# A transformer block on one core: the order of its first loads, and of its first pass over the grid

## The chip, the core and the metric

The kernel runs on one core of one Trainium2 chip. A core has five engines that run beside each other, each through its own list of instructions in order: PE (TensorE, matrix products into the PSUM accumulators), DVE (VectorE), ACT (ScalarE), POOL (GpSimd) and SP (SyncE, which here only starts transfers). Transfers between the chip's memory and the core's own SBUF are started from SP's, ACT's or POOL's list and then run on 16 DMA engines. The metric is the device time of one execution in microseconds (us), the median over several runs.

## What is computed

One layer of a diffusion backbone: 1024 tokens of 1024 features (a grid of 16 rows by 64 columns), 256 context tokens, float32 throughout. Cut to what the change touches:

```python
shift, scale, gate = adaln(c, w_ada, b_ada)          # silu(c) @ w_ada + b_ada, cut in three
shift_c, scale_c, gate_c = adaln(c_ctx, w_ada, b_ada)
h = rmsnorm(x, norm_g) * (1 + scale[:, None]) + shift[:, None]
hc = rmsnorm(ctx, norm_g) * (1 + scale_c) + shift_c
q, k, v, za, u, bg, cg, zc = jnp.split(h @ w_in, SPLIT_POINTS, axis=-1)
...
x_new = x + gate[:, None] * (jnp.concatenate([attn, conv], axis=-1) @ w_out)
```

`w_ada` is 1024 x 3072 and `w_in` 1024 x 4096. The left out lines hold a windowed attention with rotary positions and a gated short convolution.

## The kernel before

The 1024 features lie in 8 *feature tiles* of 128. Everything ahead of the first accumulator's end is called the opening here; both the change and the prediction concern it alone.

**Operands in two parts.** For float32 accuracy at the matrix unit's quicker rate, each operand of a large product is split into a high part (ACT copies it, rounding) and a low part (DVE subtracts). A product is then three matmuls: high by high, high by low, low by high. `split` does this for a slab of `w_ada`, `chunk_split` and `split_chunk(k)` for a chunk of `w_in`, `modulated` for `h`.

**adaLN.** `w_ada`'s shift and scale columns are loaded in *slabs* of 1024 rows by 256 columns, 1 MB each: `load_slab(m, j)` for m = 0..3 and j = 0 (shift) or 1 (scale). A slab pair m covers the feature tiles 2m and 2m + 1. `products(m, j)` multiplies `silu(c)` and `silu(c_ctx)` (`c2`, two columns) with a slab; for m = 0 and 1 in plain float32, which PE runs in two passes, so that one such matmul shows as two rows in the profile; for m = 2 and 3 in split form. The outcome lies in one partition per condition. `row_copy` brings it to SBUF, `modulation(m, rw)` turns it with eight small matmuls against `comb` ("turns") into a column per feature, and three DVE operations add the biases and write `ab`, the shift and scale per feature.

**x.** `load_x` loads row tiles of 128 tokens, 0.5 MB each, `xx[0..7]`; tiles 0 to 3 are *half 0* of the grid, 4 to 7 half 1. Each tile gets `square` (ACT, sum of squares), `root` (a small DVE operation, then POOL's power) and `norm` (DVE). `transposed(half, k)` turns feature tile k of four row tiles on PE into one of two `tr` banks, and `turn(half, k, engine)` applies `ab` and writes `h`'s two parts: ACT writes the high part, ACT or DVE the full value `hw`, DVE the low part.

**The first pass over the grid.** `first_columns(half, k)` multiplies chunk k of `w_in` (three columns blocks of 128) with feature tile k of one half: nine matmuls of 512 columns into three accumulators of that half. There are six accumulator banks (`acc0[u][half]`) and two `tr` banks, which fill the eight banks of PSUM. In before, the pass goes through both halves for each pair of feature tiles.

**What sets the order.** During the opening every engine, and SP with its transfers, is held to the order in which the code is written (`strict`). So an instruction that waits holds up all that is written behind it on its engine. Transfers issued from ACT or POOL are outside this rule but still stand in those engines' lists. In before SP's loads are, in order: vec and ci (the small constants and the identity), slab pair 0 in halves, x tiles 0 to 3, chunk 0, x tiles 4 to 7, chunk 1, slab pair 1, chunks 2 and 3, slab (2,0). Slabs from m = 1 on share three slots, with x's context tile `xc`, the table inputs `rw8` and the rotary table `rg` behind them; `rg` (four POOL operations in `gains`) takes the slot of slab (3,1), so it waits for the last `split`. SP stores `rg`, loads chunks for the next stage behind it, then the bias tables, then the weights `uraw`.

Of the kernel before, what the change touches and what calls it, by code (L numbers as in the profile page):

```python
# [10 lines left out]
F32 = mybir.dt.float32  # L11
# [3 lines left out]
ALU = mybir.AluOpType  # L15
# [4 lines left out]
P = 128  # L20
# [19 lines left out]
def body(tc, es, x, ctxt, w_ada, b_ada, w_in, q_g, k_g, rpbr, w_out, vecs, cst, out):  # L40
# [74 lines left out]

    vec = cp.tile([P, P], F32, name="vec")
    nvec = vecs.shape[0]
    sp.dma_start(vec[:nvec], vecs)
    sp.dma_start(ci, cst[:, 0:P + 2])
    few = cp.tile([P, 8], F32, name="few")  # L120
    pool.memset(few[:, 0:4], -0.5)
    pool.memset(few[:, 4:5], 1.0)
# [18 lines left out]
    def place(k, shape, dtype, name):  # L141

        return hpool.tile(shape, dtype, name=name, tag=f"h{k}")
# [377 lines left out]
    def tr():  # L521
        return ps0.tile([P, 512], F32, name="tr", tag="tr", bufs=2)
# [4 lines left out]
    def load_x(ts):  # L527
        for t in ts:
            xx[t] = xp.tile([P, D], F32, name="xx", tag="xx", bufs=8)
            sp.dma_start(xx[t], x[0, t * P:(t + 1) * P])  # L530

    def load_slab(m, j):

        new = place(6 + j, [P, KT, 256], F32, "slab") if m == 0 else sl.tile([P, KT, 256], F32, name="slab", tag="slab", bufs=3)
        n = 2 if m == 0 else 1
        for i in range(n):
            rows = slice(KT // n * i, KT // n * (i + 1))
            sp.dma_start(new[:, rows], bass.AP(w_ada.tensor, w_ada.offset + j * D + 256 * m + 3 * D * P * rows.start,
                                               [[3 * D, P], [3 * D * P, KT // n], [1, 256]]))
        slabs[m, j] = new  # L540

    def load_chunks(ks):
        for k in ks:
            chunks[k] = chunk_load(CU, k)

    load_slab(0, 0)
    load_slab(0, 1)
    load_x(range(4))
    load_chunks([0])
    load_x(range(4, 8))  # L550
    load_chunks([1])
# [9 lines left out]
    pv = tr()  # L561
# [32 lines left out]
    def products(m, j, kts=range(KT)):  # L594

        if m not in mods:
            mods[m] = tr()
        rows = mods[m][:2 if m < 2 else 4, 256 * j:256 * j + 256]
        parts = [(c2, slabs[m, j])] if m < 2 else [(c4, highs[j]), (c4, lows[j])]
        for i, (c, part) in enumerate(parts):  # L600
            for kt in kts:
                pe.matmul(rows, c[:, kt], part[:, kt], start=(i == 0 and kt == 0 and j == 0),
                          stop=(i == len(parts) - 1 and kt == KT - 1 and j == 1), skip_group_check=True)

    def row_copy(m):
        n = 2 if m < 2 else 4
        rw = cvp.tile([4, 512], F32, name="rw", tag="ub", bufs=2)
        act.copy(rw[:n], mods[m][:n])
        return rw[:n]

    def modulation(m, rw):
# [12 lines left out]
        dve.tensor_tensor(abk[:, 1], abk[:, 1], both(ng), ALU.mult)  # L624
# [90 lines left out]

    more_h(range(6))

    products(0, 0)
    products(0, 1)
    for t in range(4):  # L720
        square(xx[t], t)
    root(0)
    root(1)
    norm(xx[0], 0)
    root(2)
    norm(xx[1], 1)
    root(3)
    norm(xx[2], 2)
    rw = row_copy(0)
    modulation(0, rw)  # L730
    norm(xx[3], 3)
    transposed(0, 0)
    transposed(0, 1)
    square(xx[4], 4)
    root(4)
    split_chunk(0)
    turn(0, 0, dve)
    square(xx[5], 5)
    norm(xx[4], 4)
    root(5)  # L740
    turn(0, 1, dve)
    first_columns(0, 0)
    square(xx[6], 6)
    norm(xx[5], 5)
    root(6)
    square(xx[7], 7)
    norm(xx[6], 6)
    root(7)
    split_chunk(1)
    norm(xx[7], 7)  # L750
    first_columns(0, 1)
    products(1, 0, range(4))
    transposed(1, 0)
    turn(1, 0, act)
    products(1, 0, range(4, KT))
    load_slab(2, 1)
    load_chunks([4, 5])
    transposed(1, 1)
    products(1, 1)
    load_slab(3, 0)  # L760
    split_chunk(2)
    turn(1, 1, act)
    first_columns(1, 0)
    rw = row_copy(1)
    split_chunk(3)
    split(2, 0, 0)
    load_slab(3, 1)
    load_chunks([6, 7])
    transposed(0, 2)
    modulation(1, rw)  # L770
    turn(0, 2, dve)
    split(2, 0, 1)
    split(2, 1, 0)
    split(2, 1, 1)
# [3 lines left out]
    transposed(1, 2)  # L778

    for m in range(1, 4):  # L780
# [10 lines left out]
        if m == 1:  # L791
            split(3, 0, 0)
            split(3, 0, 1)
            tables = gains_load()
# [24 lines left out]
        if new:  # L819
            split_chunk(k + 3)  # L820
        if m == 1:
            split(3, 1, 0)
# [11 lines left out]
        if m == 1:  # L834
            split(3, 1, 1)
# [588 lines left out]
```

## Time and profile before

| | us |
|---|---|
| median of 3 runs | 655.83 (655.49 to 657.02) |
| profiled execution: span, first to last instruction | 653.6 |
| span not covered by the median | 2.2 (655.83 - 653.6) |
| mean granted TensorE clock over the span | 0.995 |

The profiled execution has no separate time beside its span. The profile's page gives busy time by engine, the chain of waits that ended last, and groups of instructions; a window gives busy time of each engine in a stretch of the span, the clock granted to PE, the share of the 16 DMA engines that was busy, and GB/s. A row of the timeline has start, duration, engine, line, operation, the tile written and the tile read, a count, and in brackets the idle time of the engine before it with what ended it. Nearly all rows carry line 55, a helper that records every operation, so groups are told apart by tile names: `tr`, `acc`, `xx`, `sqj` (squares), `xss` (roots), `slab`, `slabh`, `slabl`, `wr`, `wh`, `wl`, `rw`, `ab`, `h`, `hw`. PE is matmuls, PEld the loading of the stationary operand.

### The profile page before, as it was taken

The numbers are of one execution on the slowest core, as the hardware profiler recorded it, in microseconds if no ns is written. First come the engines' busy times: TensorE is split into PE (matmuls) and PEld (weight loads), VectorE is DVE, ScalarE is ACT, GpSimd is POOL, SyncE is SP. The second block draws the span as 40 slices with busy tenths as digits, with TensorE's granted clock in tenths as the row PEclk, the third lists the DMA queues.
The fourth block names the chain that finished last, engine by engine and source line by source line (L and its number), as shares of the span: only waits on it lengthen the run. The fifth ranks groups of instructions, "written<-read, shape, count | busy, mean of one in ns | idle before, by whom it ended". The sixth has DMA issues, their size and how long they took to land.

```text
span 653.6 us, 10275 instructions
## 1 busy us (share of the span) xinstructions
PE 628.5 (96%) x3469; PEld 539.0 (82%) x3469; DVE 431.8 (66%) x814; ACT 322.1 (49%) x693; POOL 129.7 (20%) x137
## 2 busy tenths in 40 slices
PE   5899998999899999999999999999999999999997
PEld 1567798999699999977878888888888888888885
DVE  1567664866584856457786989988998864575111
ACT  3566643442543534427677647565685654342000
POOL 1204102312222222101111211111211210104421
PEclk9799999999999999999999999999999999999999
DMA  8863647686586799789949586877782223966621
GB/s 320 311 210 134 169 117 232 201 259 202 143 266 196 247 276 261 188 221 215 238 106 234 143 200 174 224 188 165 212 193 78 73 74 104 316 225 206 207 100 51
DMA packets 118865, 125.46 MB, mean 192 GB/s; under 512 B 32818, under 2 KB 89354, under 8 KB 117533
## 3 DMA queue, kind: packets, MB, share of 16 engines
q1 hardware_dynamic: 112348, 113.23, 60.3%
q10 hardware_dynamic: 6208, 11.05, 5.4%
q0 software_dynamic: 256, 0.54, 0.3%
q8 instruction: 27, 0.44, 0.3%
q14 instruction: 26, 0.20, 0.1%
HBM read 88.01 MB, written 38.53 MB: 194 GB/s over the span
## 4 chain that ended last, share of the span: by engine, by line
PE 70%; DMA 10%; DVE 7%; SPq 5%; ACT 3%; issue 2%; POOL 1%; ACTq 0%; DVEq 0%; POOLq 0%
PE pu L55 20%; PE pacc L55 17%; PE po L55 5%; PE pout L76 4%; PE pout L74 4%; PE pout L75 4%; SPq L55 3%; DMA k_s<-k_d 3%; PE cacc L55 3%; PE tr L55 3%; PE pss L55 2%; PE pmx L55 2%; DMA v<-v_d 2%; DMA xx<-in_x 2%; DVE mx L55 1%
## 5 line engine op out<-in xcount | busy, mean ns | idle before, releaser
L55 PE MATMUL pu<-h,uh 128*128 128x512 f32 x544 | 169.0, 392 | 0.0
L55 PE MATMUL pacc<-wh,h 128*128 128x384 f32 x512 | 135.5, 338 | 0.6 <-ACT qn L55 0.6
L55 PEld LDWEIGHTS pu<-h,uh 128*128 128x128 f32 x544 | 98.2, 188 | 17.0
L55 PE MATMUL pu<-h,ul 128*128 128x512 f32 x272 | 106.3, 391 | 0.0
L55 PEld LDWEIGHTS pacc<-wh,h 128*128 128x128 f32 x512 | 92.9, 188 | 1.0 <-ACT qn L55 1.0
L55 POOL TENSOR_TENSOR plc<-sc,phc 128x512 fp32r<-128x512 f32 x32 | 42.4, 1324 | 222.1 <-ACT sc L55 120.0
L55 PE MATMUL pacc<-wl,h 128*128 128x384 f32 x256 | 85.6, 334 | 0.0
L55 POOL TENSOR_TENSOR ss<-ss,few 128x4 f32<-128x4 f32 (+1 forms) x40 | 41.9, 1050 | 131.6 <-DVE ss L55 131.3
L55 PEld LDWEIGHTS pu<-h,ul 128*128 128x128 f32 x272 | 51.1, 188 | 11.3
L55 DVE TENSOR_TENSOR mx<-mx,sb 128x384 f32<-128x384 f32 (+1 forms) x64 | 55.8, 880 | 2.0
L75 PE MATMUL pout<-wol,yh 128*128 128x512 f32 x128 | 49.8, 389 | 0.0
L76 PE MATMUL pout<-woh,yl 128*128 128x512 f32 x128 | 49.6, 389 | 0.0
L55 DVE TENSOR_REDUCE ss<-sq 128x4 f32<-128x260 f32 (+1 forms) x40 | 15.8, 394 | 50.3 <-ACT sq L55 50.2
L74 PE MATMUL pout<-woh,yh 128*128 128x512 f32 x128 | 48.3, 389 | 0.0
L55 PEld LDWEIGHTS pacc<-wl,h 128*128 128x128 f32 x256 | 48.1, 188 | 0.1
L55 ACT COPY mg<-pmx 128x256 f32<-128x256 f32 x32 | 12.0, 374 | 58.3 <-PE pmx L55 47.4
L55 ACT ACTIVATE sq<-pacc 128x256 f32<-128x256 f32 x32 | 12.3, 385 | 53.0 <-PE pacc L55 52.2
L1356 DVE TENSOR_TENSOR ot<-pout,gate 128x512 f32<-128x512 f32 x16 | 10.8, 688 | 38.4 <-PE pout L76 36.3
L55 DVE TENSOR_TENSOR pll<-sb,phl 128x768 fp32r<-128x768 f32 (+2 forms) x33 | 29.3, 889 | 7.9 <-ACT sb L55 7.9
L1357 POOL TENSOR_TENSOR ot<-ot,xr 128x512 f32<-128x512 f32 x15 | 20.1, 1344 | 68.2 <-DVE ot L1356 67.3
L55 DVE TENSOR_TENSOR sc<-sc,mg 128x512 f32<-128x512 f32 x32 | 21.8, 683 | 17.4 <-ACT mg L55 17.4
L55 ACT ACTIVATE qn<-pacc,ss 128x64 f32<-128x64 f32 x128 | 29.9, 327 | 6.4 <-POOL ss L55 3.2
(146 smaller groups left out, 1273.9 us busy)
## 6 DMA issues: line engine op xcount, KB each, us to landing
uraw<-in_w_in SPq DMA_DIRECT2D x34, 256.0 KB
q_d<-qs SPq DMA_DIRECT2D x64, 128.0 KB
k_s<-k_d SPq DMA_DIRECT2D x16, 512.0 KB
q_s<-q_d SPq DMA_DIRECT2D x32, 256.0 KB
wr<-in_w_in SPq DMA_DIRECT2D x40, 192.0 KB
slab<-in_w_ada SPq DMA_DIRECT2D x6, 1024.0 KB
t_d<-btw SPq DMA_DIRECT2D x8, 576.0 KB
bt<-t_d SPq DMA_DIRECT2D x8, 576.0 KB
```

What stands on the lines that cost most here:

```text
L55: i = emit(*a, **kw)
L74: i = pe.matmul(ps, ah, bh, start=first, stop=False)
L75: pe.matmul(ps, ah, bl, start=False, stop=False)
L76: pe.matmul(ps, al, bh, start=False, stop=last)
L1356: dve.tensor_tensor(ot, ps, gate[:, cols], ALU.mult)
L1357: (dve if (nh, t) == (1, NB - 1) else pool).tensor_tensor(ot, ot, xr, ALU.add)
```

## The change

Four things.

- vec and ci are loaded through ACT's list instead of SP's, and SP begins with x tiles 0 to 3.
- Slab pair 0 is loaded by feature tile: for k = 0 and 1 the shift and scale columns of that tile alone, two pieces of 0.5 MB with rows of 512 bytes instead of 1024. Products, row copy and modulation of pair 0 are done for each of the two tiles by itself (`first_products`, `first_row`, `first_modulation`). x tiles 4 to 7 come behind slab pair 1.
- The products of the pairs 0 and 1, and the first small transpose, no longer use the `tr` banks but accumulator banks of half 1, which the grid pass needs later.
- The grid pass takes half 0 through the feature tiles 0 to 3, then half 1 through the same four, and goes on as before from feature tile 4. `split_chunk`, `split`, the later loads and the squares are placed anew within that order.

```diff
-    sp.dma_start(vec[:nvec], vecs)
-    sp.dma_start(ci, cst[:, 0:P + 2])
+    act.dma_start(vec[:nvec], vecs)
+    act.dma_start(ci, cst[:, 0:P + 2])
...
+    def load_first_slabs(k):
+
+        both = place(6 + k, [P, 2, KT, P], F32, "slab")
+        for j in range(2):
+            sp.dma_start(both[:, j], bass.AP(w_ada.tensor, w_ada.offset + j * D + P * k,
+                                             [[3 * D, P], [3 * D * P, KT], [1, P]]))
+        slabs[k] = both
...
-    load_slab(0, 0)
-    load_slab(0, 1)
     load_x(range(4))
-    load_chunks([0])
-    load_x(range(4, 8))
-    load_chunks([1])
+    for k in range(2):
+        load_first_slabs(k)
+        load_chunks([k])
     load_slab(1, 0)
     load_slab(1, 1)
-    load_chunks([2, 3])
+    load_chunks([2])
+    load_x([4, 5])
+    load_chunks([3])
+    load_x([6, 7])
     load_slab(2, 0)
...
+    def first_products(k, j):
+
+        ps = mods[k] = acc0[1 - k][1]
+        for kt in range(KT):
+            pe.matmul(ps[:2, P * j:P * j + P], c2[:, kt], slabs[k][:, j, kt], start=(j == 0 and kt == 0),
+                      stop=(j == 1 and kt == KT - 1), skip_group_check=True)
+
+    def first_row(k):
+        rw = cvp.tile([4, 512], F32, name="rw", tag="ub", bufs=2)
+        act.copy(rw[:2, :256], mods[k][:2, :256])
+        return rw[:2]
...
```

The order of the opening after the change, as it is written (`first_modulation` is `modulation` for one feature tile, with four turns and three DVE operations of half the size):

```python
    for t in range(3):
        square(xx[t], t)
        root(t)
        if t:
            norm(xx[t - 1], t - 1)
            transposed(0, 0, [t - 1])
            transposed(0, 1, [t - 1])
    square(xx[3], 3)
    root(3)
    norm(xx[2], 2)
    norm(xx[3], 3)
    first_products(0, 0)
    transposed(0, 0, [2])
    transposed(0, 1, [2])
    first_products(0, 1)
    transposed(0, 0, [3])
    transposed(0, 1, [3])
    rw = first_row(0)
    split_chunk(0)
    first_modulation(0, rw)
    turn(0, 0, dve)
    first_products(1, 0)
    first_products(1, 1)
    first_columns(0, 0, (0,))
    rw = first_row(1)
    split_chunk(1)
    first_columns(0, 0, (1,))
    first_modulation(1, rw)
    turn(0, 1, dve)
    products(1, 0)
    load_slab(2, 1)
    load_chunks([4, 5])
    products(1, 1)
    load_slab(3, 0)
    square(xx[4], 4)
    root(4)
    split_chunk(2)
    square(xx[5], 5)
    norm(xx[4], 4)
    root(5)
    first_columns(0, 0, (2,))
    transposed(0, 2)
    first_columns(0, 1, (0,))
    rw = row_copy(1)
    norm(xx[5], 5)
    split_chunk(3)
    modulation(1, rw)
    turn(0, 2, dve)
    first_columns(0, 1, (1, 2))
    transposed(0, 3)
    square(xx[6], 6)
    root(6)
    turn(0, 3, act)
    first_columns(0, 2)
    square(xx[7], 7)
    norm(xx[6], 6)
    root(7)
    split(2, 0, 0)
    norm(xx[7], 7)
    split(2, 0, 1)
    transposed(1, 0)
    turn(1, 0, act)
    first_columns(0, 3)
    transposed(1, 1)
    split(2, 1, 0)
    split(2, 1, 1)
    turn(1, 1, act)
    load_slab(3, 1)
    load_chunks([6, 7])
    first_columns(1, 0)
    transposed(1, 2)
    ...
    turn(1, 2, act)
    products(2, 0)
    first_columns(1, 1)
    split(3, 0, 0)
    split(3, 0, 1)
    tables = gains_load()
    split_chunk(4)
    products(2, 1)
    rw = row_copy(2)
    transposed(1, 3)
    first_columns(1, 2, (0,))
    modulation(2, rw)
    turn(1, 3, act)
    split_chunk(5)
    split(3, 1, 0)
    first_columns(1, 2, (1, 2))
    transposed(0, 4)
    turn(0, 4, dve)
    split(3, 1, 1)
    first_columns(1, 3)
    transposed(1, 4)

    for m in range(2, 4):
        ...
```

The loop over m that follows is the one of before, without its parts for m = 1.

More of the change, by code (lines that the diff above doesn't have):

```diff
@@ L532, in load_slab @@
     def load_slab(m, j):
[L534 to L539, printed above, removed]
-        slabs[m, j] = new
+        new = sl.tile([P, KT, 256], F32, name="slab", tag="slab", bufs=3)
+        sp.dma_start(new, bass.AP(w_ada.tensor, w_ada.offset + j * D + 256 * m,
+                                  [[3 * D, P], [3 * D * P, KT], [1, 256]]))
+        slabs[m, j] = new
+    def load_first_slabs(k):
[4 more added lines that the diff above has]
+        slabs[k] = both
     def load_chunks(ks):
@@ L596, in products @@
         if m not in mods:
-            mods[m] = tr()
+            mods[m] = tr() if m > 1 else acc0[2][1]
         rows = mods[m][:2 if m < 2 else 4, 256 * j:256 * j + 256]
@@ L609, in row_copy, with first_modulation @@
         return rw[:n]
+    def first_products(k, j):
[7 more added lines that the diff above has]
+        return rw[:2]
+    def first_modulation(k, rw):
+        pm = mods.pop(k)
+        for j in range(2):
+            pe.matmul(pm[:, 2 * j:2 * j + 2], rw[:, P * j:P * j + P], comb[:2], start=(j == 0), stop=(j == 1),
+                      skip_group_check=True)
+        both = lambda v: v[:, k:k + 1].broadcast_to([P, 2])
+        abk = ab[:, k].rearrange("p (w j) -> p j w", j=2)
+        dve.tensor_tensor(abk[:, 0], pm[:, 0:2], both(bsh), ALU.add)
+        dve.tensor_tensor(abk[:, 1], pm[:, 2:4], both(b1), ALU.add)
+        dve.tensor_tensor(abk[:, 1], abk[:, 1], both(ng), ALU.mult)
     def modulation(m, rw):
@@ L716, in body @@
     more_h(range(6))
-    products(0, 0)
-    products(0, 1)
-    for t in range(4):
+    for t in range(3):
         square(xx[t], t)
[L722 to L726, printed above, removed]
+        root(t)
[4 more added lines that the diff above has]
+    square(xx[3], 3)
     root(3)
     norm(xx[2], 2)
-    rw = row_copy(0)
-    modulation(0, rw)
     norm(xx[3], 3)
-    transposed(0, 0)
-    transposed(0, 1)
+    first_products(0, 0)
[5 more added lines that the diff above has]
+    rw = first_row(0)
+    split_chunk(0)
+    first_modulation(0, rw)
+    turn(0, 0, dve)
+    first_products(1, 0)
+    first_products(1, 1)
+    first_columns(0, 0, (0,))
+    rw = first_row(1)
+    split_chunk(1)
+    first_columns(0, 0, (1,))
+    first_modulation(1, rw)
+    turn(0, 1, dve)
+    products(1, 0)
+    load_slab(2, 1)
+    load_chunks([4, 5])
+    products(1, 1)
+    load_slab(3, 0)
     square(xx[4], 4)
     root(4)
-    split_chunk(0)
-    turn(0, 0, dve)
+    split_chunk(2)
     square(xx[5], 5)
@@ L740, in body @@
     root(5)
-    turn(0, 1, dve)
-    first_columns(0, 0)
+    first_columns(0, 0, (2,))
+    transposed(0, 2)
+    first_columns(0, 1, (0,))
+    rw = row_copy(1)
+    norm(xx[5], 5)
+    split_chunk(3)
+    modulation(1, rw)
+    turn(0, 2, dve)
+    first_columns(0, 1, (1, 2))
+    transposed(0, 3)
     square(xx[6], 6)
-    norm(xx[5], 5)
     root(6)
+    turn(0, 3, act)
+    first_columns(0, 2)
     square(xx[7], 7)
@@ L748, in body @@
     root(7)
-    split_chunk(1)
+    split(2, 0, 0)
     norm(xx[7], 7)
-    first_columns(0, 1)
-    products(1, 0, range(4))
+    split(2, 0, 1)
     transposed(1, 0)
     turn(1, 0, act)
-    products(1, 0, range(4, KT))
-    load_slab(2, 1)
-    load_chunks([4, 5])
+    first_columns(0, 3)
     transposed(1, 1)
-    products(1, 1)
-    load_slab(3, 0)
-    split_chunk(2)
+    split(2, 1, 0)
+    split(2, 1, 1)
     turn(1, 1, act)
[L763 to L766, printed above, removed]
     load_slab(3, 1)
     load_chunks([6, 7])
[L769 to L774, printed above, removed]
+    first_columns(1, 0)
+    transposed(1, 2)
     xc = sl.tile([P, 2, D], F32, name="xc", tag="slab", bufs=3)
     sp.dma_start(xc, ctxt[0].rearrange("(i p) d -> p i d", p=P))
+    turn(1, 2, act)
+    products(2, 0)
     first_columns(1, 1)
-    transposed(1, 2)
-    for m in range(1, 4):
+    split(3, 0, 0)
+    split(3, 0, 1)
+    tables = gains_load()
+    split_chunk(4)
[6 more added lines that the diff above has]
+    split_chunk(5)
+    split(3, 1, 0)
+    first_columns(1, 2, (1, 2))
+    transposed(0, 4)
+    turn(0, 4, dve)
+    split(3, 1, 1)
+    first_columns(1, 3)
+    transposed(1, 4)
+    for m in range(2, 4):
         k, new, last = 2 * m, m < 3, m == 3
@@ L790, in body @@
         turn(0, k + 1, dve)
[L791 to L794, printed above, removed]
         if m == 2:
```

6 lines of the change are left out of this document (1 added, 5 removed).

## The prediction, made before the changed kernel had run

> **What bounds the kernel now.** I read the page first, then the two-microsecond windows of the opening, the chain of waits in order of time, and the timeline, engine by engine, up to 62 us.
>
> ```profile
> span 653.6 us, 10275 instructions
> PE 628.5 (96%) x3469; PEld 539.0 (82%) x3469; DVE 431.8 (66%) x814; ACT 322.1 (49%) x693; POOL 129.7 (20%) x137
> PE 70%; DMA 10%; DVE 7%; SPq 5%; ACT 3%; issue 2%; POOL 1%; ACTq 0%; DVEq 0%; POOLq 0%
> ```
>
> TensorE is the bound: busy 96% of the span and 70% of the chain that ended last. A change in the opening can be worth at most the time that PE loses there, so the windows come next (time, length, then busy time of PE, PEld, DVE, ACT, POOL, granted clock, DMA share, GB/s).
>
> ```profile
> 14.00:16.00 2.00, 0.00 (x0) 0.00 (x0) 1.48 (x4) 1.85 (x5) 1.44 (x2) 1.00 1.07 406
> 16.00:18.00 2.00, 0.90 (x8) 0.90 (x8) 1.05 (x3) 1.42 (x4) 1.63 (x2) 1.00 1.02 418
> 18.00:20.00 2.00, 1.22 (x8) 0.96 (x8) 1.59 (x6) 1.25 (x4) 0.44 (x1) 0.71 1.03 393
> 20.00:22.00 2.00, 1.98 (x7) 1.40 (x6) 1.23 (x2) 2.00 (x4) 0.29 (x1) 0.50 1.09 384
> 24.00:26.00 2.00, 1.88 (x6) 0.93 (x4) 1.27 (x4) 1.03 (x3) 0.55 (x1) 0.58 1.10 375
> 36.00:37.00 1.00, 1.00 (x6) 0.34 (x4) 0.00 (x0) 0.00 (x0) 0.00 (x0) 1.00 1.08 382
> 71.00:72.00 1.00, 1.00 (x8) 0.91 (x7) 0.10 (x1) 0.15 (x1) 0.00 (x0) 1.00 1.15 345
> ```
>
> PE does nothing from 14 to 16 us, little until 20, and runs at half the granted clock from about 18.8 to 25.7 (0.71 and 0.58 in the windows at the ends). The transfers are saturated: 4 KB rows (x) move at 418 GB/s, 1 KB rows (slabs) at 382, 512-byte rows (weight chunks) at 345.
>
> ```profile
> 5.37 9.98 DMA xx<-in_x
> ...
> 28.90 8.36 PE tr L55 x40
> 37.26 2.30 PE acc L55 x9
> 39.56 1.43 PE tr L55 x12
> ...
> 46.54 1.99 PE tr L55 x16
> 48.53 2.06 PE acc L55 x9
> ...
> 60.20 5.94 POOL rg L55 x4
> ...
> 96.89 7.34 DMA uraw<-in_w_in
> ```
>
> The chain begins with the fourth x tile, landing at 15.35, behind 2 MB of slabs. From 28.90 it is PE's own work. At 60.20 it leaves PE for POOL's rotary table, and through SP's queue reaches the weights of the next stage at 104. So the end follows two things alike: PE's progress, and the last slab split on DVE, which releases that table.
>
> **The change, part by part.** All times of the new order are put on the clock of this span. The opening's bytes are the same; only their order changes.
>
> *Loads.* The terms:
>
> ```profile
> 0.74 0.46 SPq L118 DMA_DIRECT2D vec<-in_vecs  x1
> 1.66 2.08 SPq L55 DMA_DIRECT2D slab<-in_w_ada  x4
> 3.28 0.32 PE L55 MATMUL tr<-ci,vec 56*128 56x56 f32 x1 [3.28 <-DMA ci<-in_cst]
> 4.13 0.20 ACT L55 CAST c<-c 128x16 fp32r<-128x16 f32 x1
> 5.31 8.68 PE L55 MATMUL tr<-slab,c 128*2 128x256 f32 x32 [1.71 <-DMA slab<-in_w_ada]
> ```
>
> A first 0.52 MB piece took 5.31 - 1.66 = 3.65 us from issue to use. x is now issued at 0.74, so its first tile is there at about 4.5 and, at 418 GB/s (1.25 us each), the fourth at 8.3 instead of 15.35. vec and ci go through ACT's queue, issued no later than before; beside x they can be late by some tenths. The cast that follows them ended 1.05 us after PE's turn at 3.28, so ACT is free for squares at 5.0 (5.6 if the small pieces wait on x). The first slab by feature tile, two pieces of 0.52 MB at 345 GB/s, lands at about 9.8 and 11.2, the second at 13.3 and 14.8, slab (1,0) and (1,1), at 382, at about 18 and 21, x's last four tiles by 27.
>
> *Before the first product.* Squares, roots and norms:
>
> ```profile
> 22.31 1.05 ACT L55 ACTIVATE sqj<-xx 128x1024 bf16<-128x1024 f32 x1
> ...
> 23.48 1.06 ACT L55 ACTIVATE sqj<-xx 128x1024 bf16<-128x1024 f32 x1
> ...
> 15.59 1.03 POOL L55 TENSOR_TENSOR xss<-xss,few 128x1 f32<-128x1 f32 x1 [0.17 <-DVE xss L55]
> ...
> 25.90 0.75 DVE L55 TENSOR_SCALAR xx<-xx,xss 128x1024 f32<-128x1024 f32 x1 [0.73 <-POOL xss L55]
> ```
>
> Squares go one per 1.17 us, so the second is done at 7.4; a root costs POOL 1.03 and a norm 0.75. DVE takes norm 1 behind root 2, whose square ends at 8.7: norm 1 ends near 9.7. PE's transposes of tile 1 stand ahead of the first product, so that starts at 10.0.
>
> *First products.* Feature tile 0 takes 32 rows of 128 columns, a shape that the trace has not.
>
> ```profile
> 5.69 0.13 PEld L55 LDWEIGHTS tr<-slab,c 128*2 128x2 f32 x1 [0.30 <-issue]
> 6.12 0.13 PEld L55 LDWEIGHTS tr<-slab,c 128*2 128x2 f32 x1 [0.30 <-issue]
> ...
> 8.64 4.83 PEld L55 LDWEIGHTS tr<-slab,c 128*2 128x2 f32 x23 [0.26 <-issue]
> ```
>
> Rows of 256 columns went at 0.43 us at first, and at 0.21 from 8.64, 3.4 us later. Half the columns cost 0.107 at best; a row of 256 columns in one pass costs 0.12 (16 in 1.99 above), which caps weight load and issue. I take 0.12, and 0.21 while PE is slow. The slow stretch lasted 3.4 us here and, the second time, from the first grid matmul at 20.76 to about 25.7, 4.9 us. With 4.2, PE is slow until 14.2: 16 rows 3.4, two transposes 0.3, two rows 0.4, then 14 rows 1.7. The products of feature tile 0 end at **15.8** (14.0 if PE were quick from the first row: 32 x 0.12 and 0.2; 17.1 if slow throughout).
>
> *From there to the end of products(1,1).* Row copy 0.45, four turns 0.5 (half of eight in 1.0), 32 rows for feature tile 1 3.8 (landed by 14.8), six grid matmuls 1.4 (nine take 2.06 to 2.30), four turns 0.5.
>
> ```profile
> 33.64 3.61 PE L55 MATMUL tr<-slab,c 128*2 128x256 f32 x16
> 37.30 0.58 ACT L55 COPY rw<-tr 2x512 f32<-2x512 f32 x1 [2.10 <-PE tr L55]
> 39.92 1.05 PE L55 MATMUL tr<-ci,rw 2*128 2x2 f32 x8
> 40.90 0.97 PE L55 MATMUL acc<-h,wh 128*128 128x512 f32 x3
> 41.53 0.78 ACT L55 ACTIVATE h<-tr,ab 128x512 fp32r<-128x512 f32 x1 [2.29 <-DVE ab L55]
> 42.21 2.94 ACT L55 CAST slabh<-slab 128x1024 fp32r<-128x1024 f32 x3
> ```
>
> products(1,0) and (1,1) cost twice 3.61 less their tails, 7.1. Sum 13.75, so they end at 29.55; call it Q. Without a further wait PE would here be some 3 us ahead.
>
> *The new wait.* Behind Q, ACT's order is row copy, chunk split, h(0,2), square 6, h(0,3) twice, square 7, slab split; DVE has norm 7 behind the first slab split; and PE has transposed(1,0), which needs norm 7, ahead of first_columns(0,3). Square 6 waits, in ACT's order, for h(0,2), which needs modulation(1), although x's last tiles are there from 27. From Q:
>
> ```profile
> 39.27 1.22 DVE L55 TENSOR_TENSOR slabl<-slab,slabh 128x1024 fp32r<-128x1024 f32 x1 [0.40 <-ACT slabh L55]
> 58.52 0.60 PE L55 MATMUL tr<-ci,xx 128*128 128x128 f32 x4
> ```
>
> PE: 3 grid matmuls 0.7, 4 transposes 0.36, 3 matmuls 0.7, 8 turns 1.0 = 2.8. To h(0,2): 40.90 to 41.53, 0.63. Then h 0.68 (41.53 to 42.21), square 1.17, h(0,3) 0.68 and 0.68, square 1.17, slab half 1.0 (three in 2.94), its low part 1.22, norm 0.75, last transpose 0.15. Together 10.95: PE resumes at **40.55** (call it S). Its own work in that time is 2.8 + 1.4 + 0.36 + 2.1 + 0.36 = 7.0, so it stands still about 4.0 us. What is queued behind the waiting transpose is the whole rest of the opening on PE.
>
> *Against before.* At S, PE has done 27 grid matmuls, 20 transposes, products 0 and 1 and modulation 1: the state that before reached at 40.90. From there to the end of first_columns(1,3) before took until 58.52, 17.62 us. The same work in the new order is 5 x 2.15 (nine matmuls, between 2.06 and 2.30) + 4 x 0.36 + 2 x 1.9 (products(2,0) is 1.99 with its tail) + 1.0 = 17.0; such a sum leaves out small waits, so I count half of the 0.6. The last slab split follows PE's place in both orders. Result: -0.35 - 0.3, or **-0.6 us**.
>
> *Nothing else.* One row copy on ACT and three small additions on DVE are new (the four feature columns of slab 0 are turned in two goes); together under 1.2 us, they lie beside PE's 32 rows and its products, and without that cover they would add just that. SP issues two transfers fewer, ACT two more, ahead of its table load. The accumulator banks lent to the first modulations are written by grid half 1 only after S. The 0.15 us per slab piece lost to 512-byte rows lies before data that PE is not ready for.
>
> **The rivals.** *Half clock after the stall.* The 3.1 us in which PE stood still (5.31 + 8.68 to 17.10) was followed by a granted clock of 0.50 over 6.8 us, and the slow start lasted 3.4. Grid matmuls then go at 0.48 instead of 0.23:
>
> ```profile
> 20.76 1.65 PE L55 MATMUL acc<-h,wh 128*128 128x512 f32 x3
> 22.20 1.49 PE L55 MATMUL acc<-h,wl 128*128 128x512 f32 x3
> ```
>
> A stall of 4.0 us at 36.6 is longer than that one. It costs half the slow time, 1.7 to 3.4; I take 2.2, so **657.4**. It decides if the clock falls before 44. Against it: before's cut followed only light work (eight turns, three transposes), and here dense matmuls stand on both sides. [...]
>
> *The head start survives.* If PE is quick from the first product, everything is 1.8 us earlier: 655.2 - 1.8 = **653.4**; a norm 7 that comes sooner than the sum would add to it. For it: all sums are of work that is ready. Against it: PE began slow at 5.28 after rest, and here rests longer.
>
> *The loads do not come sooner.* If ci is held up behind x, squares start at 5.6 or later, products at 10.5, and the chain ends 0.5 to 1.0 later: **656.0**. The small bytes (0.1 MB beside 2.1) speak against more.
>
> **How the numbers follow.** The sum is against a span of 653.6; the runs' median is 655.83, so 2.2 us lie around the span, and I keep them: 655.83 - 0.6 = 655.2, with a range of its own of 654.0 to 656.5. Chances: forecast 0.37, half clock 0.32, head start 0.25, loads not sooner 0.06. Beyond 0.2% (1.3 us, about what a measurement of this kernel tells from no change) lie: of the forecast 0.08 on the quick and 0.04 on the slow side, of the head start 0.23, of half clock 0.27, of the last 0.03. So faster 0.31, same 0.35, slower 0.34. Range 652.6 to 658.5: it leaves out the far ends of the two large rivals.
>
> **What would show it.** Right: first_columns(0,0) starting near 20.5 us, hardly ahead of 20.76; first products at 0.21 and then 0.12 a row; PE idle for some 4 us ahead of the transposes of x's last tile, released by a norm on DVE; POOL's table starting within 1 us of 60.2. Wrong: an idle time there under 2 us, or the table before 58; a granted clock under 1 after 36 us would show the first rival.

## The result, and the profile after

| | before | after |
|---|---|---|
| median, us | 655.84 (16 runs, 653.46 to 660.76) | 659.12 (16 runs, 656.65 to 662.81) |
| profiled execution, span, us | 653.6 | 661.0 |
| ratio of the times, 95% interval | 1 | 1.0045 (1.0027 to 1.0063) |

The change made the kernel slower, by 1.8 to 4.1 us: outside the range, and on the side that had a chance of 0.34. The executions of one kernel lie from 2.5 us below its median to 4.9 above it, and the profiled one of the changed kernel (662.81) is the slowest of its 16, so the profile has to say which part belongs to the change.

The timeline of the changed kernel, start of the opening (start, duration, engine, line, operation, tiles, in brackets the idle time before it):

```profile
0.74 1.81 SPq L55 DMA_DIRECT2D xx<-in_x  x4
...
1.43 0.37 ACTq L119 DMA_DIRECT2D ci<-in_cst  x1
...
6.25 0.32 PE L55 MATMUL acc<-ci,vec 56*128 56x56 f32 x1 [6.25 <-DMA ci<-in_cst]
...
7.11 0.21 ACT L55 CAST c<-c 128x16 fp32r<-128x16 f32 x1
7.22 1.05 ACT L55 ACTIVATE sqj<-xx 128x1024 bf16<-128x1024 f32 x1
...
10.47 0.69 PE L55 MATMUL tr<-ci,xx 128*128 128x128 f32 x2 [3.90 <-DVE xx L55]
...
12.30 3.57 PE L55 MATMUL acc<-slab,c 128*2 128x128 f32 x16
...
16.42 2.57 PE L55 MATMUL acc<-slab,c 128*2 128x128 f32 x16
...
25.67 7.07 PE L55 MATMUL acc<-slab,c 128*2 128x256 f32 x32
```

`ci` was issued at 1.43 and used at 6.25; before, issued at 1.25, it was used at 3.28. The first square follows the cast at 7.22 without waiting for x: x was there, and ACT, in its order, stood behind `c`, which needs the constants. The first product starts at 12.30, and the products of feature tile 0 end at 18.99, the first 16 rows at 0.22 us each (3.57 / 16). Q, the end of products(1,1), is 25.67 + 7.07 = 32.74.

The same timeline at the stall, and at the end of the opening:

```profile
39.69 0.39 PE L55 MATMUL tr<-ci,xx 128*128 128x128 f32 x2
...
40.91 0.33 PE L55 MATMUL tr<-ci,xx 128*128 128x128 f32 x1 [0.84 <-DVE xss L55]
...
41.47 1.23 DVE L55 TENSOR_TENSOR slabl<-slab,slabh 128x1024 fp32r<-128x1024 f32 x1 [0.55 <-ACT slabh L55]
...
42.61 0.75 DVE L55 TENSOR_SCALAR xx<-xx,xss 128x1024 f32<-128x1024 f32 x1
...
43.41 0.33 PE L55 MATMUL tr<-ci,xx 128*128 128x128 f32 x1 [2.17 <-DVE xx L55]
43.50 0.95 PE L55 MATMUL acc<-h,wh 128*128 128x512 f32 x3
...
60.60 0.60 PE L55 MATMUL tr<-ci,xx 128*128 128x128 f32 x4
...
62.28 5.93 POOL L55 TENSOR_TENSOR rg<-rw 128x512 f32<-128x512 f32 x4 [2.66 <-DVE slabl L55]
```

PE stands still for 0.84 us ahead of x's tile 6 and for 2.17 ahead of tile 7. The second wait ends with norm 7 on DVE (42.61), which stood behind the slab's low part (41.47). PE resumes at S = 43.50. POOL's table, which I take as the mark of the opening's end, starts at 62.28 instead of 60.20: **2.08 us later**.

The table is not quite the end. Behind it, ACT waits for a weight chunk of the next stage, and PE for an `h` that stands behind that chunk's cast on ACT:

```profile
75.92 0.51 ACT L55 CAST wh<-wr 128x384 fp32r<-128x384 f32 x1 [1.51 <-DMA wr<-in_w_in]
...
77.17 0.97 PE L55 MATMUL acc<-h,wh 128*128 128x512 f32 x3 [1.05 <-ACT h L55]
```

Before has no such wait there. So the first matmul of the projections, `pacc`, starts at 88.7 instead of 85.1, 3.6 us later. Such a wait, of 0.86 to 1.20 us, stands in 7 of the 12 profiled executions of the new order and in neither of the two of the old one; whether the new order causes it is not shown, and no run was aimed at it.

The rest of this execution's distance lies elsewhere. The rows by tile of the changed kernel (count, shortest/median/longest in ns, first and last start) for the first matmul behind the projections, `pmx`, and for the last stage, `pout`:

```profile
L55 PE MATMUL pmx<-ci,mx x64: 270/271/474, 295.3 to 539.2; 128*128 128x128 f32 x64
L74 PE MATMUL pout<-woh,yh x128: 389/389/389, 569.3 to 655.7; 128*128 128x512 f32 x128
```

and windows of it (time, length, busy time of PE, granted clock, DMA share, GB/s):

```profile
334.00:338.00 4.00, 2.01 (x7) 0.66 0.41 110
338.00:342.00 4.00, 4.00 (x16) 0.50 0.00 0
```

In before the same rows start at 292.9 and 561.9. So the changed kernel was 2.4 us late at 293 and 7.4 late at 562. Between them, in a stretch that the change doesn't touch, two things came together. PE stood still for 3.28 us, where the same wait in before is 0.20 (at 330.40), after ACT had waited for a transfer of v:

```profile
332.00 0.37 ACT L55 COPY mg<-pmx 128x256 f32<-128x256 f32 x1 [5.57 <-DMA v<-v_d]
...
335.71 0.97 PE L55 MATMUL pmx<-ci,mx 128*128 128x128 f32 x2 [3.28 <-DVE mx L55]
```

And the granted clock fell to 0.50 for about 6.8 us ((4 x 0.34 + 4 x 0.50) / 0.5, and 0.99 in the next four), which, reckoned from the clock, costs at most half of that. Whether this belongs to the change is the first question.

### The profile page after: what moved, and what is told of

It is laid out like the page before. It is cut to its first block, busy times and chain, and to the rows that moved or that the text cites. A ratio compares the mean times of both kernels' runs of the same rounds, so it can differ in the third digit from the quotient of the medians.

```text
span 661.0 us, 10342 instructions
## 1 busy us (share of the span) xinstructions
PE 629.8 (95%) x3501; PEld 543.0 (82%) x3501; DVE 431.2 (65%) x816; ACT 322.8 (49%) x695; POOL 130.0 (20%) x137
## 4 chain that ended last, share of the span: by engine, by line
PE 38%; DVE 5%; DMA 4%; issue 1%; ACT 1%; SPq 1%; ACTq 0%; DVEq 0%
PE pu L55 16%; PE po L55 5%; PE pout L76 4%; PE pout L74 4%; PE pout L75 4%; DMA k_s<-k_d 3%; PE pss L55 2%; PE pmx L55 2%; DVE mx L55 1%; PE pc L55 1%; DVE sb L55 1%; DVE sc L55 1%; DMA y_d<-tb 1%; DVE ul L55 0%; DVE tb L55 0%
```

## The experiments

All kernels compute the same as the changed kernel. Each has a median of 6 to 12 runs, beside runs of the kernel before on the same chip, whose medians were 655.29 to 656.65 us; kernels of different sets are compared by the ratio. The last columns are from one profiled execution each.

| kernel | median, us | ratio to before, 95% | first product | `rg` starts |
|---|---|---|---|---|
| before (above) | 655.84 | 1 | 5.31 | 60.20 |
| after (above) | 659.12 | 1.0027 to 1.0063 | 12.30 | 62.28 |
| after, again | 658.55 | 1.0003 to 1.0062 | 12.11 | 63.26 |
| constants first (SP) | 658.91 | 1.0015 to 1.0062 | 10.83 | 61.91 |
| squares early | 656.09 | 0.9974 to 1.0024 | 12.16 | 58.69 |
| both | 655.24 | 0.9967 to 1.0007 | 11.44 | 58.55 |
| norm 7 first | 657.31 | 0.9988 to 1.0038 | 11.90 | 60.48 |
| x from ACT | 657.43 | 1.0006 to 1.0062 | 11.27 | 61.60 |
| 12 matmuls at the start | 657.07 | 1.0000 to 1.0042 | 13.29 | 60.70 |
| 24 matmuls in the stall | 659.94 | 1.0039 to 1.0088 | 11.53 | 62.70 |
| both, splits early | 654.30 | 0.9959 to 0.9991 | 11.60 | 59.58 |
| both, 10 matmuls at the start | 653.82 | 0.9926 to 0.9971 | 10.95 | 58.00 |
| both, start filled | 654.27 | 0.9956 to 1.0017 | 11.15 | 55.72 |
| before, constants on ACT | 657.00 | 0.9984 to 1.0034 | 7.47 | 61.05 |

**The changed kernel again.** No edit.

> The changed kernel itself, unchanged, for a second profiled execution and a second set of times. Theory A (the opening's 2.1 us are in every execution, and the rest of the difference comes and goes from one execution to the next): ci is used near 6.3 us again, the first product is at 12.0 to 12.5, TensorE stands still for 3 to 3.5 us ahead of x's last tile, POOL's table starts between 62.0 and 62.6 (near 63.9 if half clock follows the stall in this one); the cut of the clock near 335 us is not there again; the span is under 660; the median is within 1 us of 659.1. Rival B (the change itself disturbs the middle of the program): the same cut at about 335 us, and the same 2 to 3 us lost between 320 and 400 us.

Its timeline behind the stall:

```profile
42.72 0.33 PE L55 MATMUL tr<-ci,xx 128*128 128x128 f32 x1 [2.17 <-DVE xx L55]
42.80 0.94 PE L55 MATMUL acc<-h,wh 128*128 128x512 f32 x3
43.59 1.22 PE L55 MATMUL acc<-h,wl 128*128 128x512 f32 x3
44.60 1.48 PE L55 MATMUL acc<-h,wh 128*128 128x512 f32 x3
...
63.26 5.95 POOL L55 TENSOR_TENSOR rg<-rw 128x512 f32<-128x512 f32 x4 [2.66 <-DVE slabl L55]
```

and its rows by tile:

```profile
L55 PE MATMUL pmx<-ci,mx x64: 270/271/328, 297.1 to 536.6; 128*128 128x128 f32 x64
L74 PE MATMUL pout<-woh,yh x128: 389/389/389, 566.7 to 653.1; 128*128 128x512 f32 x128
```

The late constants and the stall are there again. The long wait and the clock cut at 334 are not (1.00 from 330 to 346): rival B falls, as the distance hardly grows from 293 (4.2 us) to 562 (4.8). This time half clock follows the stall: three grid matmuls take 1.48 us instead of 0.86. From S to the first matmul of products(2,0) this execution takes 6.63 us (42.80 to 49.43) and the first one 5.05 (43.50 to 48.55): half clock costs 1.6. The opening's loss was 2.08 in one execution and 3.06 in the other; the interval of the whole time, 1.8 to 4.1, holds both.

**Constants first.** `act.dma_start` becomes `sp.dma_start`:

```diff
-    act.dma_start(vec[:nvec], vecs)
-    act.dma_start(ci, cst[:, 0:P + 2])
+    sp.dma_start(vec[:nvec], vecs)
+    sp.dma_start(ci, cst[:, 0:P + 2])
```

> Only the loads of vec and ci go back to the head of SP's list, ahead of x; all else is the changed kernel. Theory A (the small constants are held up on ACT's queue, turn by turn beside x's 4 KB rows, and that costs 2.3 us ahead of the first product): ci is used at 3.3 us instead of 6.25, the first product starts at 10.3 instead of 12.30, POOL's table at 59.3 to 60.3 instead of 62.28, and the time comes 2.0 to 2.9 us under the changed kernel, 0 to 0.9 over the kernel before. Theory B (the loss is the standstill ahead of x's last tile alone, the constants are hidden behind x's arrival): POOL's table within 0.5 us of 62.28, the time within 0.5 us of the changed kernel, 2.5 to 3.5 over before.

Its timeline:

```profile
3.35 0.32 PE L55 MATMUL acc<-ci,vec 56*128 56x56 f32 x1 [3.35 <-DMA ci<-in_cst]
...
10.83 3.57 PE L55 MATMUL acc<-slab,c 128*2 128x128 f32 x16
...
41.52 0.94 PE L55 MATMUL acc<-h,wh 128*128 128x512 f32 x3
42.30 1.23 PE L55 MATMUL acc<-h,wl 128*128 128x512 f32 x3
43.32 1.49 PE L55 MATMUL acc<-h,wh 128*128 128x512 f32 x3
```

The constants are 2.9 us earlier, and PE resumes at 41.52, 1.98 sooner. But half clock follows the stall here too, and `rg` is only 0.37 ahead of the changed kernel's. The median didn't follow (658.91). By the numbers theory B came, the table within 0.5 us of 62.28 and the time within 0.5 of 659.12, but not for its reason: first product and S did move. So the place of the 2 us is right, and their worth in the time is not shown by this run.

**Squares early.** Squares, roots and norms of tiles 6 and 7 move from behind modulation(1) to the place right behind `root(5)`, norm 5 with them:

```diff
     norm(xx[4], 4)
     root(5)
+    square(xx[6], 6)
+    norm(xx[5], 5)
+    root(6)
+    square(xx[7], 7)
+    norm(xx[6], 6)
+    root(7)
+    norm(xx[7], 7)
     first_columns(0, 0, (2,))
```

> Only the squares, roots and norms of x's tiles 6 and 7 go ahead of row_copy(1), where ACT has nothing to do from 29.5 to 32.8 us; vec and ci stay on ACT's queue. Theory A (PE's 3.5 us without work ahead of the transposes of x's last tile comes from ACT's order): the idle time ahead of them falls under 0.3 us; ACT's own order of slab splits then sets 1.2 us of it anew ahead of products(2,0), so POOL's table comes 2.3 to 3.5 us sooner, 58.8 to 60.0, and the time is 2.3 to 3.5 under the changed kernel, 0.5 over to 0.6 under before. Theory B (the standstill only takes the place of a later wait): the table stays within 0.5 us of 62.28.

Its timeline where the stall was:

```profile
38.93 0.60 PE L55 MATMUL tr<-ci,xx 128*128 128x128 f32 x4
39.28 0.94 PE L55 MATMUL acc<-h,wh 128*128 128x512 f32 x3
...
45.01 1.09 PE L55 MATMUL tr<-slabh,c 128*4 128x256 f32 x8 [0.43 <-ACT hw L55]
```

The stall is gone, 0.43 us of it return ahead of products(2,0), `rg` starts 3.59 us sooner (0.76 of it lay ahead of Q in this execution, 24.91 + 7.07 = 31.98), and the median falls by 3.0 us to that of before; in the same set of runs it is 2.8 under the kernel with the constants first. Of the single edits this one moves the time most: the stall alone is about as large as the loss. That the table is 1.5 us ahead of before's and the time is not fits the wait behind the table, 0.97 us here too: the first `pacc` starts at 85.0, where before has 85.1.

**Both.** The two edits together.

> Both edits together. Theory A: the two losses follow each other on PE, so they add: 4.3 to 6.4 us under the changed kernel, 1.4 to 3.5 under before, POOL's table at 56.5 to 58. If they cover one another, it is no better than the better of the two alone.

The median is 655.24, but the edits don't add: `rg` gains 0.14 us over the squares alone. `ci` is used at 3.35, but the third x tile lands late (its square waits 0.87 us for it), the first product is at 11.44, and the slow rows last until about 16.9. So of the 2.3 us by which the first product was late, only 0.9 came back in this execution, and Q (24.78 + 7.07 = 31.85) is hardly ahead of that with the squares alone.

**Norm 7 first.** `norm(xx[7], 7)` changes places with `split(2, 0, 0)`.

> The changed kernel with norm(xx[7], 7) ahead of split(2, 0, 0) instead of behind it. Theory A (the chain to the last transposes of x's tiles goes through DVE's order: norm 7 stands behind the slab's low part, 1.23 us): norm 7 starts some 1.1 us sooner, TensorE resumes near 42.3 instead of 43.5, the stall is about 2.3 us, POOL's table starts near 61.1, and the median is 657.5 to 658.5. Rival B (the squares on ACT set it, and the slab's split fills a wait only): TensorE resumes within 0.4 of 43.5 and the time stays at 659.1.

Its timeline:

```profile
41.61 0.33 PE L55 MATMUL tr<-ci,xx 128*128 128x128 f32 x1 [1.22 <-DVE xx L55]
...
60.48 5.95 POOL L55 TENSOR_TENSOR rg<-rw 128x512 f32<-128x512 f32 x4 [2.69 <-DVE slabl L55]
```

PE waits 1.22 us for norm 7 instead of 2.17, and Q was 0.8 sooner in this execution (24.83 + 7.07 = 31.90). From Q to S it takes 9.80 us, 0.96 less: theory A holds in the opening. The median, 657.31, is 1.2 under the changed kernel's in the same set, but the intervals overlap, so the time doesn't decide. DVE's order was 1 us of the stall; the rest goes when the squares move too (the run with squares early), which fits ACT's order, square 6 behind h(0,2).

**Before, with constants on ACT; and x from ACT.** The first takes the kernel before and issues vec and ci from ACT. The second takes the changed kernel and exchanges the queues:

```diff
-    def load_x(ts):
+    def load_x(ts, queue=sp):
...
-            sp.dma_start(xx[t], x[0, t * P:(t + 1) * P])
+            queue.dma_start(xx[t], x[0, t * P:(t + 1) * P])
...
-    load_x(range(4))
+    load_x(range(4), act)
```

with vec and ci at the head of SP's queue.

> The kernel before, with only vec and ci moved to ACT's queue; SP then begins with the first slabs, 1 KB rows. Theory A (ci gets one 512-byte piece for each piece of the other queue, so what it waits is set by the size of those pieces, 0.16 us for 4 KB and 0.046 for 1 KB): ci is used at 3.3 to 4.2 us, the first product starts under 6.0 us, and the time is within 0.5 us of before, since x's fourth tile at 15.35 hides it. Theory B (a load from ACT's queue is slow as such): ci at about 6, the first product at 7 or later.

> The changed kernel with the queues exchanged: x's first four tiles are issued from ACT, vec and ci from SP at the head of its queue, with the slabs behind them. Theory A (what ACT issues lands late beside a long row of transfers on SP's queue): ci is used at 3.3 to 3.6 us, as in the kernel before, but x's tiles, on ACT's queue, land late: the first square starts at 6 or later and the fourth x tile is there at 12 or later. Rival B (a small transfer beside a long queue is held up, whichever engine issues either): ci is used at 6 us or later again, and x lands as in the changed kernel, with its squares right behind the cast at 7.2. Rival C (the queues share alike, and only the order of issue counted): ci at 3.3 to 3.6 and the first square at 5.0 to 5.5. The time within 1.5 us of the changed kernel's by all three.

In the first, `ci` is used at 6.59 although SP's pieces have rows of 1 KB: the expected 3.3 to 4.2 fell, and theory B's late arrival came (first product at 7.47). That opening ends 0.85 us later, which the time doesn't show (0.9984 to 1.0034). In the second, with the small transfers on SP's queue and x on ACT's, it is used at 5.21, between the 3.3 to 3.6 of theories A and C and the 6 of B, and x isn't late: the first square follows the cast at 6.18. So theory A of that run falls, and with it the slow queue of the run before: it is not ACT's queue as such. The view of the transfers shows what happens. For the changed kernel, from 5 to 6 us (q1 is SP's queue, q10 ACT's; packets, MB, share of the 16 engines):

```profile
q1 hardware_dynamic: 93, 0.32, 79.5%
q10 hardware_dynamic: 144, 0.07, 23.7%
```

From 4 to 5 us it has no packet of q10, and 0.39 MB of q1. For the exchanged queues, from 4 to 5 us:

```profile
q10 hardware_dynamic: 103, 0.41, 100.7%
q1 hardware_dynamic: 29, 0.01, 4.9%
```

So the small transfers move little while another queue's large packets fill the engines, whichever queue has which: from 4 to 5 us nothing beside packets that took 100.2% of the engines in the changed kernel, and 0.01 MB beside 100.7% with the queues exchanged. With all of these loads on SP's queue and the small ones ahead, `ci` is used at 3.21 to 3.37 in the seven kernels that have it so. What in the DMA engines orders it so was not tried.

**Matmuls at the start and in the stall.** Matmuls of the identity by itself, into an idle bank, ahead of the first products (12), or ahead of the transposes of x's last tiles (24, with the constants first):

```diff
+    for _ in range(12):
+        pe.matmul(acc0[1][1][:, :P], ident, ident, start=True, stop=True)
```

> The changed kernel with 12 matmuls of the identity by itself (into a bank that is free then) put on TensorE right behind the first transpose, so that it doesn't rest between 6.6 us, where ci lands, and the first products at 12.3. What is computed is the same. Theory A (the first products went slowly until about 17.2 us because TensorE had rested before): with work from 6.6 on the slow pace ends by about 11, the 32 rows of feature tile 0 take about 4.5 us instead of 6.7, and the products of feature tile 0 end near 16.8 instead of 19.0; everything behind is 1.5 to 2.3 us earlier, POOL's table starts near 60.2 instead of 62.3, and the median is 657.2 or so, 1.5 to 2.3 under the changed kernel, unless the stall before x's last tile is again followed by half clock. Rival B (the slow pace belongs to rows of 128 columns at the start, by weight load or by the landing of the slabs): the rows still take 6.7 us, the end of them is at 19 or later, and the time is that of the changed kernel, 659.1, within 0.5.

> The changed kernel with vec and ci back at the head of SP's queue, and with 24 matmuls of the identity by itself ahead of the transposes of x's last tiles, in the stall, about 2.8 us of work at full clock, into a bank that is free then. What is computed is the same. Theory A (in the kernel with the constants first, the half clock behind the stall, 42.5 to 45.9 us, came from the stall, and it gave back most of what the earlier constants brought): the granted clock stays full behind the stall, the first grid matmuls behind it take 0.94 to 0.85 per three and not 1.23 to 1.49, POOL's table starts near 60.3 instead of 61.9, and the median is 1 to 1.6 us under that kernel's 658.9. Rival B (the cut comes by itself, as those at 177 and 331 us do): the matmuls behind the stall are slow in this profile too or the median doesn't move by more than 0.5; the added work then costs up to 0.3.

Each matmul is two passes, which I hadn't counted. The timeline of the twelve:

```profile
7.34 5.49 PE L55 MATMUL acc<-ci 128*128 128x128 f32 x24
12.62 0.73 PE L55 MATMUL tr<-ci,xx 128*128 128x128 f32 x4
13.29 1.91 PE L55 MATMUL acc<-slab,c 128*2 128x128 f32 x16
```

The first product is 1.0 us later, mostly because `ci` came later in this execution (used at 7.09 instead of 6.25). Yet all its rows then take 0.12 us, and the products of feature tile 0 end at 17.41 instead of 18.99: the slow pace does not belong to the shape, and rival B falls. Theory A's cause, PE's rest, fits this execution; that it is the cause is not shown (see the ten matmuls below). The median is 657.07, where theory A had 657.2, but its interval overlaps the changed kernel's, so the trace carries this point and not the time. The 24 in the stall lasted 5.5 us instead of 2.8 and made the opening longer, so that their time (659.94) says nothing on the clock's price. Three grid matmuls behind them take 0.93, 0.84 and 0.85 us, at a granted clock of 1.00 (42 to 48 us). The first execution of the changed kernel had 1.00 there without such matmuls, so that they kept the clock up is not shown.

**Towards a quicker kernel.** Three more on top of both edits: `split(2, 0, 0)` ahead of modulation(1) and its second half behind; ten matmuls at the start; and twelve of them, placed to leave PE hardly a rest.

> The changed kernel with vec and ci at the head of SP's queue, the squares and norms of x's tiles 6 and 7 ahead of the rest of first_columns(0,0), and the two halves of the first slab split on either side of modulation(1). Theory A (the opening's end is set by TensorE's progress and by the last slab split, which follows it): the wait of 0.4 us ahead of products(2,0) goes too, POOL's table starts between 57.5 and 58.5, 2 us ahead of the kernel before, and the median is 654 to 655.2, the fastest of all. Rival B (ACT's casts of the slab, now ahead of h(0,2), hold up h and so TensorE by the 1.0 us that they take): TensorE waits some 1 us ahead of first_columns(0,2), the table starts near 59, and the median is 655.5 to 656.5, not under the kernel with the two other edits alone (655.2).

> The changed kernel with vec and ci at the head of SP's queue, the squares and norms of x's tiles 6 and 7 ahead of the rest of first_columns(0,0), and 10 matmuls of the identity by itself right behind the first transpose, in time in which TensorE has nothing else to do (each is two passes of 0.21 us, as the twelve showed, so 4.3 us, from 3.7 to about 8.0, ahead of the first transposes at 8.7). What is computed is the same. Theory A (slow pace after rest, in the first products, is what is left of the loss): the rows of feature tile 0 go at 0.12 us soon after the first product at 11.4, its products end near 15.6 instead of 17.8, POOL's table starts between 56.2 and 57.2, 3 to 4 us ahead of the kernel before, and the median is 652.5 to 654. Rival B (the transfers: slabs that land late hold the products once they are quick, or the rest between the transposes makes TensorE slow again): the products of feature tile 0 end at 17 or later, the table starts near 58.5, and the median is that without the ten matmuls, 655.2, within 0.6.

> The kernel with both edits and ten matmuls of the identity, with an eleventh there and one more between the transposes of x's first and second tile, so that TensorE has work nearly without a gap from 3.6 us to the first products (the ten left 0.8 and 0.5 us of rest at 8.3 and 9.7, and the products were slow until about 17 all the same). What is computed is the same. Theory A (the full pace comes after about 5.5 us of work without a rest, as behind the twelve matmuls that ended at 12.6, and any rest starts that anew): the first products at 11 go at 0.12 us a row from the start, those of feature tile 0 end near 15.3 instead of 17.8, POOL's table starts between 55.5 and 56.8, and the median is 651.5 to 653. Rival B (the full pace comes at a time of its own, which the work ahead of it doesn't move much): the products are slow until 15 to 17 again, the table starts near 58, and the median is 653.8 within 0.6. Rival C (quick products run into the slabs' landing): rows quick at first, then waits on a slab's transfer, the table at 57 to 58.

With the early splits rival B's wait came (1.38 us ahead of first_columns(0,2), on ACT's h) and `rg` started at 59.58, yet the median is theory A's, 654.30. With ten matmuls PE worked without a gap from 3.6 to 8.2, and the first products were slow all the same (3.57 us for 16 rows). The opening is rival B's, the table at 58.00, and the median, 653.82, is theory A's: the two don't agree, and why is open. The timeline of that kernel:

```profile
3.62 4.63 PE L55 MATMUL acc<-ci 128*128 128x128 f32 x20
9.02 0.69 PE L55 MATMUL tr<-ci,xx 128*128 128x128 f32 x2 [0.77 <-DVE xx L55]
...
10.95 3.57 PE L55 MATMUL acc<-slab,c 128*2 128x128 f32 x16
```

With the start filled they were quick, and the table came at theory A's time, though not by its mechanism; the timeline of that kernel:

```profile
3.46 4.08 PE L55 MATMUL acc<-ci 128*128 128x128 f32 x22
8.73 0.44 PE L55 MATMUL tr<-ci,xx 128*128 128x128 f32 x2 [1.20 <-DVE xx L55]
...
11.15 1.91 PE L55 MATMUL acc<-slab,c 128*2 128x128 f32 x16 [0.35 <-DMA slab<-in_w_ada]
...
55.72 5.94 POOL L55 TENSOR_TENSOR rg<-rw 128x512 f32<-128x512 f32 x4 [3.80 <-DVE slabl L55]
```

PE still rests for 1.20 and 0.98 us ahead of these transposes and stays quick, so in this execution rests of that length didn't start the slow pace anew. It was quick from 6.4 on (its first 12 passes end at 6.39, the other 10 at 7.54), in work that the kernel with ten matmuls has too, where all 20 passes were slow. So what brought the pace is not the two matmuls more; the executions differ.

This opening ends 4.5 us ahead of before's, the median only 1.0, short of theory A's, and a ratio of 1 lies within its interval. The lead is 5.3 us at the first `pmx` (287.6) and 2.5 at the first `pout` (559.4). What was given back in this execution, 2.8 us, is about a wait of 1.16 us for `mx` at 325.94, which before doesn't have, and a clock cut behind it (0.80, 0.50 and 0.85 from 326 to 332, 1.7 us). Whether a kernel that is ahead there meets that wait more often stays open. The kernel with both edits and ten matmuls, at 0.9926 to 0.9971 of before, has the lowest median and is quicker than both kernels; the one with the early splits (0.9959 to 0.9991) can't be told apart from it.

## Why the prediction was wrong

- **The failed step is the loads' term**: "beside x they can be late by some tenths", with squares at 5.0, at worst 5.6. They were at 7.22, and the first product at 12.30 instead of 10.0: 2.3 us. The worst case was no bound. The rows at hand gave one: the fourth x tile was due at 8.3, and small transfers that had to wait for all of x would have put squares some 1.05 us behind that.
- **The slow pace, the term of 4.2 us, was 5.4**, from 12.30 until about 17.7. The 32 rows and two transposes took 6.7 us instead of 5.8: 0.9 more. That it is not the shape the twelve matmuls show (0.12 a row behind them). That it comes from PE's rest, as the prediction has it, is not shown: behind the ten, 4.63 us of work, the rows still took 0.22.
- **The sums of ready work held.** From there to Q 13.75 predicted, 13.75 measured; that it fits to the digit is luck, since the 32 rows took 0.2 less and the six grid matmuls 0.2 more. From Q to S 10.95 (on 29.55 that is 40.50, where the text has 40.55), measured 10.76; the wait is the one described, by norm 7 behind the split and square 6 behind h(0,2), with 3.0 us of idle PE where the text had 4.0. From S to the last transposes of feature tile 3 17.0, measured 17.10. The errors add up to 2.3 + 0.9 - 0.2 + 0.1 = 3.1: by the full sum (-0.35 and -0.62) the table was due at 59.2, and it started at 62.28.
- **The rivals.** "The loads do not come sooner" was right in kind and mispriced: 0.5 to 1.0 for 2.3, at a chance of 0.06, since "the small bytes speak against more". Bytes were the wrong measure: the small transfers waited (no packet of theirs from 4 to 5 us), they didn't take long (0.07 MB from 5 to 6). "Half clock after the stall" was absent from the first profile and there in the second, at 1.6 us, under the 1.7 to 3.4 given; what decides whether the clock falls no run shows, and the chance of 0.32 was my estimate. "The head start survives" didn't come by itself: quick first rows (1.91 us for 16) came only in the two profiled executions that had 24 passes of the identity ahead of them, and not in the one that had 20 (3.57).
- **Together**, the late constants, the slow pace and the stall make the table 2.1 us late without half clock and 3.1 with it; the wait behind the table, which the sum had at nothing, makes it 3.6 and 4.7 at the first `pacc`. The stall was in the sum, as the price of a head start of some 3 us; the head start was what didn't come. In the time, only the stall's price is shown: its removal brought 3.0 us. Constants in time brought little by themselves (658.91), so what the failed term costs in the whole time stays open.

## What to carry to other kernels

A small transfer that everything waits for goes ahead of the large ones on the same queue; here `ci` was used at 3.21 to 3.37 us so, and at 5.21 to 7.09 on another queue beside them. So that is not free, and its own bytes don't bound it; I take the end of what is in flight as the bound, an estimate that no run here went beyond. When a loop is turned round, look for what the new order puts behind the first late instruction on each engine: here two squares and the norms behind them, written a few lines sooner, gave back the whole loss. A head start won from transfers counts only as far as PE can use it: the first 16 rows took 3.57 us in the changed kernel, and 1.91 behind the twelve matmuls, so the slow pace is priced with it.

## What the runs showed that was not expected

- PE's slow pace at the start stands in no record of the clock: in the changed kernel the granted clock reads 1.00 in every us from 12 to 17, while a pass of 128 columns takes 0.22 us (3.57 / 16), and 0.12 behind the twelve matmuls (1.91 / 16).
- The full pace came some 3.2 us after work began in one execution (first work at 3.21, quick from 6.4) and had not come after 4.6 us of unbroken work in another (20 passes from 3.62), nor after 5.5 in a third (24 passes from 7.34). What sets the moment no run shows.
- Behind the same stall, half clock came in some executions and not in others: the granted clock was 0.50 from 44 to 46 us in the second of the changed kernel and with the constants first, and from 42 to 44 with x from ACT; it was 1.00 from 40 to 48 in the first of the changed kernel and with the twelve matmuls. What decides it no run shows.
- Cuts of the clock to 0.50 also came near 180 us (0.50 from 180 to 182 with the constants first, 1.00 in the first execution of the changed kernel), or between 327 and 342 (0.50 from 338 to 342 in that execution, 1.00 in the second), where PE waits briefly (in before it is busy 0.66 of 2 us from 176, and 3.03 of 4 from 330). They come and go from one execution to the next, and the executions of the changed kernel lie between 656.65 and 662.81, so a single profile can be several us away from the median without the edit having any part in it.
